# A branch after expert 0 that gives four experts two blocks instead of two, with three- and two-block experts in turn

## The chip, the cores and the metric

The kernel runs on one core of one Trainium2 chip. Its time is the device time of one execution in microseconds (us); the kernel before takes 1819.07 us, the median of 3 runs from 1818.38 to 1819.39.

## What is computed

The reference is a two-layer model over 256 latent tokens and 256 context tokens of width 1024. Layer 0 is neighbourhood attention and a dense SwiGLU; layer 1 is differential attention and a mixture of eight experts, of which each token takes two. A final RMSNorm ends it. The part that matters here is the mixture:

```python
def moe_swiglu(h, w_router, w_gate, w_up, w_down):
    logits = (h @ w_router).astype(jnp.float32)
    top_vals, top_idx = lax.top_k(logits, TOP_K)          # TOP_K = 2 of N_EXPERTS = 8
    top_w = jax.nn.softmax(top_vals, axis=-1)
    gates = jnp.sum(jax.nn.one_hot(top_idx, N_EXPERTS, dtype=jnp.float32) * top_w[..., None], axis=-2)
    y = jnp.zeros_like(h)
    for e in range(N_EXPERTS):
        y = y + gates[..., e:e + 1] * swiglu(h, w_gate[e], w_up[e], w_down[e])
    return y
```

An expert has three matrices of 1024 x 3584 in float32 (D_FF_EXPERT = 3584), 42 MB in all (an MB here is 1,048,576 bytes), and the eight of them are 336 MB of weights that are read once. 256 tokens with two experts each make 512 rows, 64 for an expert on average.

## The kernel before, in words

**Stages.** The attention of both layers and the dense SwiGLU come first; the expert stage starts at about 900 us. It computes only the rows that an expert was given. The router's choice becomes a rank of each token within its expert; `dispatch` (L1379) builds a 0/1 matrix from ranks, `gather` (L1410) multiplies the tokens by it into `xg`, and `scatter` (L1438) takes the expert's output back to the tokens' rows with the transposed matrix.

**Blocks.** An expert's rows are held in blocks of 32. `BLOCKS` (L34) gives the number of blocks for each place in the order: six experts have three blocks, 96 rows, and the last two have two blocks, 64 rows. `first_gates` (L1461) counts the tokens of each expert and sorts: expert 0 is always first, the others follow by falling count. The indices go into registers of SP (L1478), from which the loads of the later experts take their addresses. If an expert got more rows than its blocks hold, an extra pass at the end (`tc.If(over > 0)`, L1650) handles the rest.

**Matmuls.** The 32 columns of a block are the stationary side, a quarter of the array at a time, and 256 columns of weights move past them. `quarters` (L1517) writes four such matmuls, one to each quarter. A unit of weights is a tile of 128 x 2048 float32, 1 MB; each unit takes two rounds of `quarters` per block, so 8 matmuls for each block: 24 with three blocks, 16 with two. The trace records two matmuls for each of these, so a unit of a two-block expert is x32 there, and one of a three-block expert x48.

**Steps of an expert.** An expert has four steps `j` (L1564 on): three with 4 units of `egate` and 4 of `eup`, and one with 4 units of `eboth`; the down projection of a step (`edown`, 4, 4, 4 and 2 units) stands one step later, so that expert `e` does the last down projection of expert `e - 1`. That makes 42 units an expert. Between them stand the transposes of the step before (L1533), and in steps 0 to 3 the dispatch of the next expert, the two halves of the scatter of the one before, and the gather of the next. TensorE, ScalarE and VectorE follow the order in which the code is written (`tc.manual_schedule`, L1564).

**The load queue.** All weights are loaded by SP, in the order of one list of units. `raw_unit` (L250) loads as far ahead as the ring of buffers is long: 17 buffers of 1 MB in the expert stage (3 + 4 + 4 + 2 + 4, L1089, L1248, L1292). A load waits until TensorE has used the unit that lay in its buffer. Loads take eight completion semaphores in turn, and a load also waits until the one that used its semaphore before has landed, so at most eight are in flight. L206 is the load's line; a tile `w` in the rows is a unit.

**The end.** The last expert's rows go straight through `last_expert` (L1610) into `final_norm` (L1626): squares on ScalarE, products on POOL, then four output transfers, two issued by SP and two by ScalarE (L1643). Then every engine loads a register and branches over the extra pass (L1649, L1650).

Of the kernel before, what the change touches and what calls it, by code (L numbers as in the profile page):

```python
# [17 lines left out]
D = 1024  # L18
# [11 lines left out]
NE = 8  # L30
# [3 lines left out]
BLOCKS = (3, 3, 3, 3, 3, 3, 2, 2)  # L34
# [139 lines left out]
class Stream:  # L174
# [4 lines left out]
    def __init__(self, nc, units, ahead, hl_pool, n_hl):  # L179
        self.nc, self.units = nc, units  # L180
        self.index = {u[0]: i for i, u in enumerate(units)}
        self.ahead = ahead
        self.rings, self.count = {}, {}
        self.hl_pools = [(hl_pool, n_hl)] * n_hl
        self.loaded = self.split = self.offset = self.nh = 0
        self.raw, self.hl = {}, {}

    def ring(self, name, *pools):

        self.rings[name] = [p for p in pools for _ in range(p[1])]  # L190
        self.count.setdefault(name, 0)

    def load_to(self, n):
        while self.loaded < min(n, len(self.units)):
# [5 lines left out]
            ring = self.rings[name]  # L200
            pool, bufs, tag = (*ring[self.count[name] % len(ring)], "w32")[:3]
            if pool is None:
                return
            self.count[name] += 1
            t = pool.tile([128, UNIT], F32, name="w32", tag=tag, bufs=bufs)
# [4 lines left out]
    def piece(self, n):  # L210

        while self.split < min(n, len(self.units)):
# [4 lines left out]
            self.load_to(i + 1 + len(self.rings[name]))  # L217
# [51 lines left out]
def body(tc, A, out):  # L269
# [65 lines left out]
    place = []  # L335

    def at_place(n, r, u):
        if not r:
            return A[n][0, u]
        return A[n][bass.ds(place[r - 1], 1), u].rearrange("a p c -> (a p) c") if place else None  # L340

    def add_expert(n, r, u0, nu):
        for u in range(u0, u0 + nu):
            add((n, r, u), lambda u=u: at_place(n, r, u), UNIT, False)

    steps = [(e, j) for e in range(NE) for j in range(4)]
    for i in range(len(steps) + 1):
        if i < len(steps):
            e, j = steps[i]
            if j < 3:  # L350
                add_expert("egate", e, *ESTEPS[j])
                add_expert("eup", e, *ESTEPS[j])
            else:
                add_expert("eboth", e, 0, 4)
        if i:
            e, j = steps[i - 1]
            add_expert("edown", e, 4 * j, 4 if j < 3 else 2)
# [6 lines left out]
    with ExitStack() as top:  # L364
# [1012 lines left out]
        slots_of = [32 * b for b in BLOCKS]  # L1377

        def dispatch(e, r, n):  # L1379

            d = adas[:, 256 * (e % 2):256 * (e % 2) + 2 * n].rearrange("p (b s) -> p b s", b=2)
# [4 lines left out]
        def slots(e, d, n):  # L1386

            p = PT.tile(None, None, "o")
            for tb in range(2):
                PE.transpose(p[:n, 128 * tb:128 * tb + 128], d[:, tb], ident)  # L1390
            scat[e] = scats[e % 3]
            SC.copy(scat[e][:n], p[:n, :256])

        def gather_half(hf, d, u, tag, n):

            p = PT.tile(None, None, tag)
# [13 lines left out]
        def gather(e):  # L1410
            xg[e] = ep.tile([128, KC, 96], F32, name="xg", bufs=2)
            for hf in range(2):
                gather_half(hf, dis[e], xg[e], ("o", "pt")[hf], slots_of[e])
# [12 lines left out]
        def collect(e, pd):  # L1426

            n = slots_of[e]
            oe = ep.tile([128, D], F32, name="oe", bufs=1)
# [8 lines left out]
        def scatter(e, hf):  # L1438

            c = slice(512 * hf, 512 * hf + 512)  # L1440
            n = slots_of[e]
            for tb in range(2):
                p = PT.tile(None, None, ("o", "pt")[tb])
# [4 lines left out]


# [4 lines left out]
        dis[0] = dispatch(0, rks, slots_of[0])  # L1454
# [3 lines left out]
        cnti = mp.tile([128, 1], I32, name="cnti")  # L1458
        ordi = mp.tile([128, 8], I32, name="ordi")

        def first_gates():  # L1461
            slots(0, dis[0], slots_of[0])

            pk = PT.tile(None, None, "o")
# [12 lines left out]
            with nc.allow_non_contiguous_dma("registers"):  # L1477
                place.extend(nc.values_load(ordi[0:1, r:r + 1], engines=[mybir.EngineType.SP], min_val=0,  # L1478
                                            max_val=NE - 1) for r in range(1, NE))
# [31 lines left out]
            V.tensor_copy(cnti, key[:, 0, 0:1])  # L1511
# [214 lines left out]
```

## Time and profile before

| | |
|---|---|
| median of 3 runs | 1819.07 us |
| profiled execution | 1817.93 us |
| its span, first to last instruction | 1816.2 us |
| TensorE busy | 1753.1 us, 97% |
| VectorE, ScalarE, POOL busy | 812.7, 495.7, 83.6 us |
| moved by DMA | 488.77 MB, mean 269 GB/s |
| expert matmuls, gate and up (L1520) | 9856 x 379 ns |
| expert matmuls, down (L1520) | 4928 x 379 ns |
| mean granted clock of TensorE | 0.995 |

The durations of single matmuls overlap, since they are pipelined, so what a unit costs is read from the starts of the groups that follow each other, and not from the mean of 379 ns. A stage of the expert part can be limited by TensorE or by the loads, and the page's averages don't tell which; the stretches by expert and the waits do.

### The profile page before, as it was taken

What the parts mean: (1) busy time and instruction counts of PE and PEld (TensorE: products, weight loads), DVE (VectorE), ACT (ScalarE), POOL (GpSimd) and SP (SyncE); (2) the same over time, 40 slices, a digit from 0 to 9 for tenths busy, and PEclk for the clock granted to TensorE, in tenths of its full rate; (3) what the DMA queues carried; (4) which work ended last, traced back from release to release, by engine and by line L of the source; (5) the groups of instructions that cost most, each with busy time, mean ns of one, the idle gap of its engine ahead of it and who ended that gap; (6) DMA issues with size and microseconds to landing.
All of it is one profiled execution on the core that took longest, in us unless ns stands there. A gap on an engine that the chain in (4) does not pass through costs nothing. (4 is left out here: it accounts for less than half of the span.)

```text
span 1816.2 us, 46890 instructions
## 1 busy us (share of the span) xinstructions
PE 1753.1 (97%) x20841; PEld 1269.2 (70%) x20841; DVE 812.7 (45%) x1732; ACT 495.7 (27%) x971; POOL 83.6 (5%) x133
## 2 busy tenths in 40 slices
PE   6999999999999999999999999999999999999975
PEld 4888879877778899888856556556665565565632
DVE  5688778776766767899610020200211102011202
ACT  3677664422222255666300000000000000000101
POOL 0111002000000012211000000000000000000001
PEclk9999999999999999999999999999999999999998
DMA  8334344544555354222799999999999999999995
GB/s 343 120 133 140 111 151 164 185 171 172 202 185 185 135 190 169 89 72 104 294 381 394 347 394 359 372 389 350 378 362 383 378 364 373 381 375 417 418 418 217
DMA packets 70130, 488.77 MB, mean 269 GB/s; under 512 B 8128, under 2 KB 8384, under 8 KB 13856
## 3 DMA queue, kind: packets, MB, share of 16 engines
q1 hardware_dynamic: 67824, 480.06, 69.1%
q0 software_dynamic: 1808, 5.11, 0.9%
q8 instruction: 165, 2.70, 0.6%
q10 hardware_dynamic: 288, 0.52, 0.1%
q14 instruction: 45, 0.37, 0.1%
HBM read 484.62 MB, written 1.05 MB: 267 GB/s over the span
## 5 line engine op out<-in xcount | busy, mean ns | idle before, releaser
L1520 PE MATMUL ps_mm<-w,xg 128*32 128x256 f32 x9856 | 546.7, 379 | 6.5 <-DMA w<-eup 2.6
L1520 PEld LDWEIGHTS ps_mm<-w,xg 128*32 128x32 f32 x9856 | 315.9, 110 | 222.9 <-issue 5.6
L1520 PE MATMUL ps_s<-w,aT 128*32 128x256 f32 x4928 | 273.7, 379 | 6.6 <-DMA w<-edown 6.6
L1520 PEld LDWEIGHTS ps_s<-w,aT 128*32 128x32 f32 x4928 | 158.9, 110 | 116.0 <-DMA w<-edown 11.5
L360 PE MATMUL ps_mm<-hH,wHL 128*128 128x512 f32 (+1 forms) x616 | 230.7, 377 | 2.9 <-ACT hH L586 2.8
L362 PE MATMUL ps_mm<-hH,wHL 128*128 128x512 f32 (+1 forms) x616 | 228.7, 372 | 1.0 <-DVE wHL L230 1.0
L361 PE MATMUL ps_mm<-hL,wHL 128*128 128x512 f32 (+1 forms) x616 | 228.7, 373 | 0.0
L230 DVE TENSOR_TENSOR wHL<-w,wHL 128x1024 fp32r<-128x1024 f32 (+1 forms) x156 | 174.6, 1127 | 79.0 <-ACT wHL L229 78.5
L1542 DVE COPY aT<-ps_pt 128x384 f32<-128x384 f32 (+1 forms) x32 | 16.8, 524 | 431.5 <-PE ps_pt L1541 431.5
L229 ACT CAST wHL<-w 128x1024 fp32r<-128x1024 f32 (+1 forms) x156 | 149.9, 966 | 175.9 <-PE ps_mm L362 141.3
L360 PEld LDWEIGHTS ps_mm<-hH,wHL 128*128 128x128 f32 x616 | 115.3, 188 | 27.6 <-ACT hH L586 4.3
L362 PEld LDWEIGHTS ps_mm<-hH,wHL 128*128 128x128 f32 x616 | 115.6, 188 | 23.0 <-DVE wHL L230 1.5
L361 PEld LDWEIGHTS ps_mm<-hL,wHL 128*128 128x128 f32 x616 | 115.6, 188 | 20.7 <-DVE hL L587 0.9
L417 DVE SCALAR_TENSOR_TENSOR acc<-w,sil,acc 128x1024 f32<-128x1024 f32 x98 | 120.1, 1279 | 0.0
L1588 DVE TENSOR_TENSOR es<-es,ps_mm 128x512 f32<-128x512 f32 x24 | 16.5, 688 | 223.3 <-PE ps_mm L1520 223.3
L1573 ACT ACTIVATE es<-ps_mm 128x512 f32<-128x512 f32 x24 | 14.3, 598 | 336.8 <-PE ps_mm L1520 336.7
L360 PE MATMUL ps_mm<-aH,wHL 128*128 128x256 f32 (+1 forms) x264 | 85.1, 322 | 0.0
L361 PE MATMUL ps_mm<-aL,wHL 128*128 128x256 f32 (+1 forms) x264 | 85.0, 322 | 0.0
L362 PE MATMUL ps_mm<-aH,wHL 128*128 128x256 f32 (+1 forms) x264 | 84.4, 320 | 0.0
L360 PE MATMUL ps_mm<-wHL,hH 128*128 128x256 f32 x256 | 73.1, 285 | 0.9 <-DVE rt L1110 0.9
L361 PE MATMUL ps_mm<-wHL,hH 128*128 128x256 f32 x256 | 71.7, 280 | 0.1
L362 PE MATMUL ps_mm<-wHL,hL 128*128 128x256 f32 x256 | 71.6, 280 | 0.0
(301 smaller groups left out, 2170.4 us busy)
## 6 DMA issues: line engine op xcount, KB each, us to landing
w<-edown SPq DMA_DIRECT2D x112, 1024.0 KB, 7.5
w<-egate SPq DMA_DIRECT2D x96, 1024.0 KB, 7.2
w<-eup SPq DMA_DIRECT2D x96, 1024.0 KB, 7.2
w<-ada SPq DMA_DIRECT2D x48, 1024.0 KB, 4.9
w<-eboth SPq DMA_DIRECT2D x32, 1024.0 KB, 7.7
w<-qkv SPq DMA_DIRECT2D x24, 1024.0 KB, 4.9
w<-gu SPq DMA_DIRECT2D x22, 1024.0 KB, 4.9
w<-dn SPq DMA_DIRECT2D x24, 704.0 KB, 4.0
```

Source lines behind the costliest of these rows:

```text
L229: self.nc.scalar.copy(h[:, :n_], r[:, c])
L230: later(lambda: self.nc.vector.tensor_sub(l[:, :n_], r[:, c], h[:, :n_].bitcast(F32)))
L360: PE.matmul(o, sH, mH, start=start, stop=False)
L361: PE.matmul(o, sH, mL, start=False, stop=False)
L362: PE.matmul(o, sL, mH, start=False, stop=stop)
L417: V.scalar_tensor_tensor(acc[v], wk, x, acc[v], op0=OP.mult, op1=OP.add)
L1520: PE.matmul(out[32 * g:32 * g + 32, b0:b0 + 256], lhs(g), rhs[:, c0 + 256 * g:c0 + 256 * g + 256], start=start, stop=False, tile_position= ...
L1542: (SC.copy if q else V.tensor_copy)(t[:, q, :nb], p[:, :128 * nb].rearrange("p (b s) -> p b s", b=nb))
L1573: SC.activation(s[:, :512], pa, AF.Silu)
L1588: V.tensor_mul(s[:, :512], s[:, :512], pc)
```

## The change

`BLOCKS` becomes two tables, and `ORDER` says in which order the ranked experts run. Table 0 has four experts of three blocks and four of two; table 1 has six and two as before. Both orders begin with expert 0, and three- and two-block experts follow each other in turn (table 1 has fewer two-block experts to put between). Expert 0's four steps are common. Then all engines read the count of the fifth expert (`cnti[0]`) and branch: at 64 or fewer the rest of the kernel runs with table 0, else with table 1. Each side of the branch holds the code of all seven experts left, of the last one's scatter and of the final norm. So that both sides start from the same buffers, ring buffers, PSUM banks and the tiles `es`, `aT`, `xg` and `oe` are allocated once and taken by index.

```diff
-BLOCKS = (3, 3, 3, 3, 3, 3, 2, 2)
+BLOCKS = ((3, 3, 3, 3, 2, 2, 2, 2), (3, 3, 3, 3, 3, 3, 2, 2))
+ORDER = ((0, 7, 1, 6, 2, 5, 3, 4), (0, 7, 1, 2, 6, 3, 4, 5))
...
+    def buffer(self, name):
+        ring = self.rings[name]
+        i = self.count[name] % len(ring)
+        pool, bufs, tag = (*ring[i], "w32")[:3]
+        if pool is None:
+            return None
+        self.count[name] += 1
+        if (name, i) in self.fixed:
+            return self.fixed[name, i]
+        t = pool.tile([128, UNIT], F32, name="w32", tag=tag, bufs=bufs)
+        if name == "moe":
+            self.fixed[name, i] = t
+        return t
...
-            self.load_to(i + 1 + len(self.rings[name]))
+            self.load_to(i + bool(need) + len(self.rings[name]))
...
-            r0 = 0
-            while r0 < NE:
-                r1 = r0 + BLOCKS.count(BLOCKS[r0])
-                V.tensor_scalar(key[:, 4, r0:r1], key[:, 3, r0:r1], -float(slots_of[r0]), 0.0, op0=OP.add, op1=OP.max)
-                r0 = r1
+            V.tensor_copy(cnti[:, 0:1], key[:, 3, 4:5])
+            V.memset(caps[:, 0:6], 96.0)
+            V.memset(caps[:, 6:8], 64.0)
+            V.tensor_scalar(key[:, 4, 0:1], key[:, 3, 4:5], 64.0, -32.0, op0=OP.is_le, op1=OP.mult)
+            V.tensor_scalar(caps[:, 4:6], caps[:, 4:6], key[:, 4, 0:1], None, op0=OP.add)
+            V.tensor_sub(key[:, 4], key[:, 3], caps)
+            V.tensor_scalar(key[:, 4], key[:, 4], 0.0, None, op0=OP.max)
...
-        with tc.manual_schedule(engines={mybir.EngineType.PE, mybir.EngineType.Activation, mybir.EngineType.DVE}):
-            for i, (e, j) in enumerate(steps):
-                nb = BLOCKS[e]
+        def run(i0, i1):
+            for i in range(i0, i1):
+                e, j = at(i)
+                t = steps[i][0]
+                n_ = order[t + 1] if t + 1 < NE else None
+                l_ = order[t - 1] if t else None
+                nb = blocks[e]
...
-        fin = wp.tile([128, UNIT], F32, name="w32", tag="w32", bufs=2)[:, :D]
-        nc.sync.dma_start(fin, A["rows"][0:1].to_broadcast([128, D]))
-        def final_norm(y, z, halves):
+        def final_norm(y, halves):
+            fin = st.buffer("moe")[:, :D]
+            nc.sync.dma_start(fin, A["rows"][0:1].to_broadcast([128, D]))
+            z = st.buffer("moe").rearrange("p (b d) -> p b d", b=2)
...
+        first_gates()
+        with tc.manual_schedule(engines=pes):
+            run(0, 4)
+        def rest(a):
+            blocks[:], order[:] = BLOCKS[a], ORDER[a]
...
+            st.order(units[:dense_units] + expert_units(order))
+            with tc.manual_schedule(engines=pes):
+                run(4, len(steps))
+            i = len(steps) - 1
+            transposes(i)
+            down(i)
+            final_norm(y, last_expert(order[-1], pds.pop(order[-1])))
+        fourth = nc.values_load(cnti[0:1, 0:1], min_val=0, max_val=S)
+        with tc.If(fourth < 65) as few:
+            rest(0)
+        with few.Else():
+            rest(1)
-        over = nc.values_load(cnti[0:1, 0:1], min_val=0, max_val=S)
+        over = nc.values_load(cnti[0:1, 1:2], min_val=0, max_val=S)
         with tc.If(over > 0):
```

**On TensorE, the start of the second expert.** The names are the output tile, the weights (`w`, a unit) and the stationary side (`aT` or `xg`); `ps_s` is the down projection, `ps_mm` gate and up. Before:

```order
L1520 MATMUL ps_s<-w_9782,aT 32x256 x24
L1520 MATMUL ps_s<-w_9808,aT 32x256 x24
L1520 MATMUL ps_mm<-w_9846,xg 32x256 x24
L1520 MATMUL ps_mm<-w_9872,xg 32x256 x24
L1520 MATMUL ps_mm<-w_9898,xg 32x256 x24
L1520 MATMUL ps_mm<-w_9924,xg 32x256 x24
L1541 MATMUL ps_pt<-con,es 128x128 x3
```

The same place with the change, on the side of table 0:

```order
L1560 MATMUL ps_s<-w_8833,aT_9030 32x256 x24
L1560 MATMUL ps_s<-w_8835,aT_9030 32x256 x24
L1710 TENSOR_LOAD cnti
L1711 COMPARE_AND_BRANCH
L1560 MATMUL ps_mm<-w_8837,xg_9033 32x256 x16
L1560 MATMUL ps_mm<-w_8839,xg_9033 32x256 x16
L1560 MATMUL ps_mm<-w_8841,xg_9033 32x256 x16
L1560 MATMUL ps_mm<-w_8843,xg_9033 32x256 x16
L1581 MATMUL ps_pt<-con,es_9029 128x128 x3
```

The second expert now has 16 matmuls to a unit and not 24, and between it and expert 0's third down projection stand the register load and the branch. The code of table 0 follows the branch directly.

**On SP, the loads at the same place.** A row is a load into a ring buffer, an ISA row sets a register of the load's address. With the change:

```order
L224 DMA w_8831<-eup 128x2048
L224 ISA
L224 DMA w_8833<-eup 128x2048
L1710 TENSOR_LOAD cnti
L1710 ISA x2
L1717 TENSOR_LOAD cnti
L1717 ISA x2
L1711 COMPARE_AND_BRANCH
L224 ISA
L224 DMA w_8835<-eup 128x2048
L224 ISA
L224 DMA w_8837<-eup 128x2048
```

Before, nothing stands between those loads, and the register for the extra pass is loaded in expert 6. The branch is SP's place in its own list: it stands behind the load that goes into the buffer of the last unit but one which TensorE uses ahead of its own branch.

**On SP, the end.** Before, the output transfers and then one compare:

```order
L206 DMA w_17904<-edown 128x2048
L1624 DMA w_18198<-rows 128x1024
L1643 DMA out<-w_18200 128x512 x2
L1650 COMPARE_AND_BRANCH
```

With the change, the end of table 0's side, and the first rows of table 1's side, which a jump passes over before the compare at L1718 is reached:

```order
L224 DMA w_8849<-edown 128x2048
L1667 DMA w_8851<-rows 128x1024
L1684 DMA out<-w_8853 128x512 x2
L1711 UNCONDITIONAL_BRANCH
L224 ISA
L224 DMA w_8835<-eup 128x2048
```

The jump is new, and 562 rows of SP lie between it and the compare.

## Rows read from the trace of the kernel before

**Rows 1.** The page: TensorE's line, and its slices, DMA's and the rate.

```profile
PE 1753.1 (97%) x20841; PEld 1269.2 (70%) x20841; DVE 812.7 (45%) x1732; ACT 495.7 (27%) x971; POOL 83.6 (5%) x133
...
PE   6999999999999999999999999999999999999975
...
DMA  8334344544555354222799999999999999999995
GB/s 343 120 133 140 111 151 164 185 171 172 202 185 185 135 190 169 89 72 104 294 381 394 347 394 359 372 389 350 378 362 383 378 364 373 381 375 417 418 418 217
```

**Rows 2.** Stretches by expert 1, 5, 6, 7; last columns: clock, DMA share, GB/s.

```profile
1014.92:1134.13 119.21, 118.38 (x2084) 72.34 (x2080) 17.01 (x36) 8.04 (x18) 0.00 (x0) 1.00 0.96 376
...
1491.73:1610.87 119.14, 118.33 (x2083) 72.30 (x2079) 16.83 (x36) 7.93 (x18) 0.00 (x0) 1.00 0.97 372
1610.87:1695.06 84.19, 83.25 (x1437) 50.85 (x1433) 15.03 (x32) 6.14 (x14) 0.00 (x0) 1.00 1.01 412
1695.06:1781.44 86.38, 74.50 (x1243) 39.92 (x1235) 11.72 (x22) 4.49 (x9) 0.00 (x0) 1.00 1.01 418
```

**Rows 3.** TensorE in order of time: start, duration; three-block, then two-block units.

```profile
1065.48 10.54 PE L1520 MATMUL ps_s<-w,aT 128*32 128x256 f32 x192
1075.84 10.54 PE L1520 MATMUL ps_mm<-w,xg 128*32 128x256 f32 x192
...
1647.62 7.09 PE L1520 MATMUL ps_s<-w,aT 128*32 128x256 f32 x128
1654.53 7.09 PE L1520 MATMUL ps_mm<-w,xg 128*32 128x256 f32 x128
```

**Rows 4.** SP's waits, 1134 to 1253 us: total, times, longest.

```profile
SPq L206 <- PE ps_mm L1520: 58.8, 24, 6.5
```

**Rows 5.** Loads, KB and us to landing: 1134 to 1253; waits and loads after 1620.

```profile
w<-edown SPq DMA_DIRECT2D x14, 1024.0 KB, 7.1
...
SPq L206 <- DMA w<-edown: 31.4, 17, 2.0
...
w<-edown SPq DMA_DIRECT2D x10, 1024.0 KB, 19.8
```

**Rows 6.** TensorE in order of time, one unit a row; brackets: wait before it.

```profile
1728.73 1.93 PE L1520 MATMUL ps_mm<-w,xg 128*32 128x256 f32 x32 [1.78 <-DMA w<-eup]
...
1793.45 1.93 PE L1520 MATMUL ps_s<-w,aT 128*32 128x256 f32 x32 [0.46 <-DMA w<-edown]
```

**Rows 7.** Two stretches once the loads set the pace.

```profile
1620.00:1720.00 100.00, 99.87 (x1751) 60.69 (x1743) 19.97 (x41) 7.14 (x17) 0.00 (x0) 1.00 1.01 418
1720.00:1780.00 60.00, 49.08 (x784) 25.24 (x787) 5.47 (x9) 2.26 (x5) 0.00 (x0) 1.00 1.01 419
```

**Rows 8.** Lines L1478, L1649, L1650: duration ns min/median/max, first and last start.

```profile
L1478 SPq TENSOR_LOAD <-ordi x7: 263/263/472, 907.9 to 911.5; - x7
...
L1649 PEldq TENSOR_LOAD <-cnti x1: 483/483/483, 1800.1 to 1800.1; - x1
...
L1650 SPq EVENT_SEMAPHORE  x8: 17/17/17, 1814.0 to 1814.5; - x8
...
L1650 POOLq COMPARE_BRANCH  x1: 45/45/45, 1805.3 to 1805.3; - x1
L1650 POOLq EVENT_SEMAPHORE  x1: 17/17/17, 1805.8 to 1805.8; - x1
L1650 SPq COMPARE_BRANCH  x1: 53/53/53, 1809.8 to 1809.8; - x1
L1650 ACTq COMPARE_BRANCH  x1: 54/54/54, 1811.1 to 1811.1; - x1
L1650 ACTq EVENT_SEMAPHORE  x1: 17/17/17, 1814.3 to 1814.3; - x1
```

**Rows 9.** The end in order of time: a late weight load, the last outputs.

```profile
1801.63 0.33 PEld L1618 LDWEIGHTS ps_mm<-oe,oL 64*128 64x128 f32 x1 [0.52 <-issue]
...
1808.93 0.83 SPq L1643 DMA_DIRECT2D out<-w  x2
```

More of the change, by code (lines that the diff above doesn't have):

```diff
@@ L179, in __init__ @@
     def __init__(self, nc, units, ahead, hl_pool, n_hl):
-        self.nc, self.units = nc, units
-        self.index = {u[0]: i for i, u in enumerate(units)}
+        self.nc = nc
+        self.order(units)
         self.ahead = ahead
-        self.rings, self.count = {}, {}
+        self.rings, self.count, self.fixed = {}, {}, {}
         self.hl_pools = [(hl_pool, n_hl)] * n_hl
@@ L186, in __init__, with order @@
         self.raw, self.hl = {}, {}
+    def order(self, units):
+        self.units = units
+        self.index = {u[0]: i for i, u in enumerate(units)}
     def ring(self, name, *pools):
@@ L334, in body, with of_rank, expert_units, some @@
     ring = "moe"
-    place = []
-    def at_place(n, r, u):
+    expert = []
+    def of_rank(n, r, u):
         if not r:
             return A[n][0, u]
[L340 to L344, printed above, removed]
+        return A[n][bass.ds(expert[r - 1], 1), u].rearrange("a p c -> (a p) c") if expert else None
     steps = [(e, j) for e in range(NE) for j in range(4)]
[L347 to L357, printed above, removed]
+    def expert_units(order):
+        new = []
+        def some(n, r, u0, nu):
+            new.extend(((n, r, u), lambda u=u: of_rank(n, r, u), UNIT, False, "moe") for u in range(u0, u0 + nu))
+        for i in range(len(steps) + 1):
+            if i < len(steps):
+                e, j = steps[i]
+                if j < 3:
+                    some("egate", order[e], *ESTEPS[j])
+                    some("eup", order[e], *ESTEPS[j])
+                else:
+                    some("eboth", order[e], 0, 4)
+            if i:
+                e, j = steps[i - 1]
+                some("edown", order[e], 4 * j, 4 if j < 3 else 2)
+        return new
+    dense_units = len(units)
+    units += expert_units(ORDER[0])
     def mm3(o, sH, sL, mH, mL, start, stop):
@@ L1447, in scatter @@
                 add_rows(e, p, tb, c)
+        turn_of = {e: t for t, e in enumerate(order)}
         rk1 = mp.tile([128, 2, 8], F32, name="rk1")
@@ L1476, in first_gates @@
             V.tensor_copy(ordi, key[:, 2])
-            with nc.allow_non_contiguous_dma("registers"):
-                place.extend(nc.values_load(ordi[0:1, r:r + 1], engines=[mybir.EngineType.SP], min_val=0,
-                                            max_val=NE - 1) for r in range(1, NE))
+            expert.extend(nc.values_load(ordi[0:1, r:r + 1], engines=[mybir.EngineType.SP], min_val=0,
+                                         max_val=NE - 1) for r in range(1, NE))
             pm = mp.tile([128, 8, 8], F32, name="pm")
@@ L1528, in gate_up @@
                     k = 2 * (u0 + u) % KC + x
-                    for b in range(BLOCKS[e]):
+                    for b in range(blocks[e]):
                         quarters(ps[b], cols[b], lambda g: xg[e][:, k, 32 * b:32 * b + 32], r, D * x,
@@ L1578, in body @@
                     transposes(i - 1)
-                if j == 0 and e + 1 < NE:
-                    dis[e + 1] = dispatch(e + 1, rks, slots_of[e + 1])
-                    slots(e + 1, dis[e + 1], slots_of[e + 1])
-                elif j in (1, 2) and e:
-                    scatter(e - 1, j - 1)
-                elif j == 3 and e + 1 < NE:
-                    gather(e + 1)
+                if j == 0 and n_ is not None:
+                    dis[n_] = dispatch(n_, rks, slots_of(n_))
+                    slots(n_, dis[n_], slots_of(n_))
+                elif j in (1, 2) and l_ is not None:
+                    scatter(l_, j - 1)
+                elif j == 3 and n_ is not None:
+                    gather(n_)
                 if j < 3:
```

133 lines of the change are left out of this document (72 added, 61 removed).

## The prediction

> **What bounds the kernel now.** I read the page's busy times and slices first, then the stretches by expert, then TensorE's order of time, the waits of the load queue (SP), and the end. The page shows TensorE busy for 97% of the span, and from slice 21 of 40 to the last but one the DMA engines at 9 tenths as well, moving 347 to 418 GB/s [rows 1]. Two engines that are both nearly full call for a look stage by stage. In the expert stage five experts of three blocks take 119.2 us each and move about 372 GB/s. Expert 6, with two blocks, takes 84.2 us at 412 GB/s, and expert 7 takes 86.4 us at 418 GB/s with TensorE busy for only 74.5 of them [rows 2]. TensorE's clock is 1.00 throughout. TensorE's own order gives the price of one load of 1 MB ("unit", 42 to an expert): four units of a three-block expert take 10.36 us from start to start (1065.48 to 1075.84), 2.59 us a unit; four of a two-block expert 6.91 (1647.62 to 1654.53), 1.73 us a unit [rows 3]. The remaining 10 us of an expert are transposes, gather and scatter.
>
> With three blocks TensorE sets the pace: SP waits on it for a free buffer [rows 4], and a load lands 7.1 us after issue. At the end it is the other way round: SP waits on its own earlier loads, a load lands 19.8 us after issue [rows 5], and TensorE waits before unit after unit for its weights [rows 6]. Between the starts at 1728.73 and 1793.45 stand 26 units, 2.489 us each. That is the price of a unit when loads alone set the pace, and the rate says that the loads ran at it from about 1620 us on: 418 GB/s up to 1720, while TensorE still had stock, and 419 after that [rows 7]. So for long stretches I take 2.489 x 419/418 = 2.495 us.
>
> So at three blocks loads have 119.2 - 42 x 2.495 = 14.4 us to spare in each expert and lose them, because all 17 buffers of the ring are full. At two blocks TensorE is faster than the loads by 104.8 - 84.2 = 20.6 us an expert, and lives on the buffers.
>
> **What the change does to this.** The inputs are fixed by the reference. Worked out with its own router, the experts get 78, 71, 71, 61, 61, 66, 51 and 53 tokens. Expert 0 is first by rule, then 71, 71, 66, 61, 61, 53, 51: the fifth has 61, which is not over 64, so the branch with four two-block experts is taken, and no count exceeds its room (96 or 64), so the extra pass is skipped as before. Two experts lose one block of three, each 42 x (2.59 - 1.73) = 36 us of matmuls, and the experts run 3, 2, 3, 2, 3, 2, 3, 2.
>
> TensorE alone: from the start of the second expert (1014.92) to the last transposes (1781.44) it took 766.5 us. With three more three-block experts, three two-block ones and a last one at its busy time, 3 x 119.2 + 3 x 84.2 + 74.5 = 684.7, that is 81.8 less. This isn't the answer, since the loads then can't keep up.
>
> Loads alone: at 1610.87, before expert 6, TensorE had used 40 + 5 x 42 = 250 units, and the last of 336 was there at 1793.45, 182.6 us later; so some (1793.45 - 1610.87)/2.489 = 73.4 were outstanding and 12.6 lay landed and unused. Expert 7 of the change begins at 1014.92 in the same state (ring full behind a three-block expert, two blocks ahead) with 40 units used. From there loads need the same 182.6 us plus five experts' more, 210 units x 2.495 = 524.0, provided they never stop. They don't: the stock of 12.6 landed units goes to 4.4 after the first two-block expert (42 used, 84.2/2.495 = 33.8 landed), 10.2, 2.0, 7.8, 0, 5.8, then to zero in the last one. It never comes back to 12.6, where full buffers stopped loads before. With the old schedule the same five experts took 595.95 us, so the loads end 72.0 us earlier. TensorE, 81.8 earlier by itself, has some 10 us of slack, which hides the small edits inside its stages: other sizes of gather and scatter (the same matmul counts), five short VectorE instructions more while the tokens are counted (VectorE is busy 17 of 119 us in an expert [rows 2]), a load that is issued after the register loads of the order rather than ahead of them (the ring is full there, and three-block work covers it). If that cover went, each would cost no more than its own length, under 1 us.
>
> **The branch itself.** Each engine loads a register and compares after expert 0's last step; nothing waits there for another engine's present work, since the count was written some 100 us before (the order of the experts, worked out just ahead of it, is read at 907.9 us [rows 8]). The end of the old kernel has the same pair of instructions: TensorE's register load took 0.48 us, and ScalarE and SP stood 3.2 and 4.2 us from their compare to their next instruction (1811.1 to 1814.3, 1809.8 to 1814.0), while POOL, which jumps over a few instructions, went on after 0.5 [rows 8]. All those jumps were taken. The new one falls through into code that follows it, which no row shows: between nothing and 4.2 us. On TensorE the register load ran at 1800.1 while weights for matmuls issued earlier still loaded at 1801.63 [rows 8, 9], so about 1.5 us of sequencer work lies under matmuls already queued; on SP the queue holds some three loads. I take 0.5 us, next to POOL's row, and keep 0 and 4.2 for the range. Queued behind SP's compare are the next loads; behind TensorE's the matmuls of the second expert, whose late buffers would delay loads once that stock in flight is used up.
>
> In the Trainium skill, "Runtime: NRT & Kernel Launch", section "Instruction fetch mechanics", a taken branch to code outside the window being fetched stalls the sequencer, and fetching ahead is purely sequential. By it the fall-through costs nothing, and the sum is 0.5 less. The rows of taken jumps agree (0.5 us near, 3.2 to 4.2 far); no row shows a fall-through.
>
> At the end each engine now jumps over the other branch's code, and then over the extra pass as before. SP's part of that code is 562 rows long in the order of the program, so I price the jump at SP's 4.2 us, and it stands on the path: SP's last output transfer is issued at 1808.93 to 1809.76 [rows 9], its jump follows, and its last waits come behind it. Bounds: 0.5 (near) to 4.2.
>
> **Sum.** Own time of the profiled execution 1817.93 (span 1816.2 and 1.7 around it) - 72.0 + 0.5 + 4.2 = 1750.6. The median of the runs is 1.14 above that execution: 1751.8.
>
> **Rivals.** (a) The loads don't hold their pace. What decides is whether 2.495 us a unit lasts 700 us; the trace shows it for 170. The only long stretch, five experts, ran at 119.2/42 = 2.838 us a unit, 372 GB/s [rows 2]. If that were the loads' own limit over long times, 283.4 outstanding units would take 804 us, and the kernel 1014.9 + 804 + 22.8 (from the last landing to the end) + 4.7 + 2.9 = 1849, slower than before; the turning point is (1793.45 - 4.7 - 1014.92)/283.4 = 2.73 us a unit, 384 GB/s. Against it: in that stretch SP waited for buffers, not for loads [rows 4].
> The Trainium skill, "DMA: Bandwidth & Descriptors", section "Where 436 GB/s comes from", lets HBM bind loads at about 358 GB/s a core; that would be 2.93 us a unit and 1875. Rows 7 contradict it on this chip with one core at work (418 and 419 GB/s), and the page's own 425 GB/s for a 16 MB transfer does too.
> (b) The other branch is taken, if the chip's router counted otherwise or the counts came over 64: 22 blocks as before, but with the two-block experts spread so that TensorE never starves. That saves the 86.4 - 74.5 = 11.9 us of waiting, pays 4.2 for each taken jump and some 5 for a last expert of three blocks: about 1820, no change. Against it: 61 is four tokens from the limit.
> (c) The branch is dear: a fetch stall of about 4.2 us on SP and TensorE with the ring full, so the loads run dry: 1755.5.
> (d) The end's second jump is hidden or near, and loads hold 2.489: 1751.8 - 4.2 - 1.3 = 1746.
>
> **How the numbers follow.** Forecast 0.72, (c) 0.12, (d) 0.11, (a) 0.03, (b) 0.02. Own bounds of the forecast: pace 2.489 to 2.509 us (1,048,576 bytes at the 418 GB/s of [rows 7]) over 210 units, -1.3 to +2.9; the end -3.7 to 0; the branch -0.5 to +3.7: about 1746 to 1758. For pauses of the ring that I haven't seen I widen to 1744 to 1764. What can be told from no change is about 0.2%, 3.6 us. Faster 0.96, same 0.015, slower 0.025.
>
> **What would show it.** Right: the DMA row of the page at 9 in all slices from the second expert on, 412 to 420 GB/s in two- and three-block experts alike, SP waiting for loads more than for TensorE, TensorE waiting for weights near the end, and its last matmul of the last expert about 72 us earlier. SP's compare at the first branch should have its next load within 1 us, and the last instructions some 4 us later behind the outputs than before. Wrong: stretches under 400 GB/s with TensorE waiting for weights (a), five experts at 119 us (b), a gap on TensorE and in the DMA rate at about 1015 us (c), or SP waiting for buffers in three-block experts, which would mean that the ring filled and loads stopped again.

## The result, and the profile after

The changed kernel takes 1764.71 us, the median of 4 runs (1764.14 to 1766.74), against 1818.72 (1818.37 to 1819.39) for the kernel before: a ratio of 0.9705, 95% interval 0.9688 to 0.9721. The forecast was 1751.8 with a range up to 1764; the direction was right, the gain 13 us smaller than said. The profiled execution took 1764.36 us (span 1762.4), 53.6 us less than the one of before, where the sum had 67.3.

The table-0 side is taken, the experts alternate, and the page looks as forecast. TensorE's line, the slices of DMA's busy share, and its rate, to be held against [rows 1]:

```profile
PE 1684.8 (96%) x19483; PEld 1227.7 (70%) x19483; DVE 805.6 (46%) x1721; ACT 491.8 (28%) x963; POOL 83.6 (5%) x133
...
DMA  9243333644474446322569999999999999999993
GB/s 353 94 152 130 115 138 115 249 155 166 172 263 160 148 162 216 102 73 73 192 279 417 372 413 418 417 418 417 418 419 417 419 418 419 418 414 412 409 420 133
```

The stretches by expert, of the second to the fourth and of the last three (columns as in [rows 2], clock, DMA share and GB/s last):

```profile
1017.68:1102.19 84.51, 83.38 (x1438) 51.04 (x1438) 15.14 (x32) 6.25 (x14) 0.00 (x0) 1.00 1.01 416
1102.19:1221.40 119.21, 118.53 (x2086) 72.69 (x2082) 15.00 (x32) 7.93 (x18) 0.00 (x0) 1.00 1.01 418
1221.40:1305.70 84.30, 81.98 (x1401) 49.52 (x1394) 15.14 (x32) 6.21 (x14) 0.00 (x0) 1.00 1.01 418
...
1423.01:1519.70 96.69, 86.87 (x1437) 49.22 (x1430) 15.14 (x32) 6.22 (x14) 0.00 (x0) 1.00 1.01 418
1519.70:1638.90 119.20, 118.52 (x2082) 73.73 (x2086) 15.01 (x32) 7.93 (x18) 0.00 (x0) 1.00 1.01 414
1638.90:1736.16 97.26, 84.44 (x1406) 45.09 (x1398) 13.98 (x27) 4.49 (x9) 0.00 (x0) 1.00 0.94 385
```

A three-block expert still takes 119.2 us, but now at 414 to 418 GB/s and not 372 to 376. The two-block experts grow from 84.5 to 97 us, because TensorE comes to wait for weights. From 1017 to 1740 us SP waits for its own earlier loads (504 us in the first four rows) and little for TensorE (the fifth row is the largest of these), and a load lands 20.1 us after issue where it took 7.1 [rows 5]:

```profile
SPq L224 <- DMA w<-edown: 166.5, 87, 2.8
SPq L224 <- DMA w<-egate: 143.8, 72, 2.9
SPq L224 <- DMA w<-eup: 140.5, 72, 2.9
SPq L224 <- DMA w<-eboth: 52.7, 26, 2.8
SPq L224 <- PE ps_mm L1560: 31.2, 43, 3.3
```

So loads set the pace, as forecast; the pace is what came out slower. Two units for which TensorE waited, the 166th and the 336th (the last) of the expert stage:

```profile
1303.12 1.94 PE L1560 MATMUL ps_s<-w,aT 128*32 128x256 f32 x32 [0.56 <-DMA w<-edown]
...
1736.16 1.93 PE L1560 MATMUL ps_s<-w,aT 128*32 128x256 f32 x32 [0.55 <-DMA w<-edown]
```

Between these starts lie 170 units and 433.04 us, 2.547 us each, where the 26 units of [rows 6] had 2.489. Neighbouring starved units still stand 2.48 to 2.49 apart; single ones come later.

**Where the 13.7 us between sum and result lie.** The second expert starts at 1017.68 and not 1014.92 (+2.8, not in the sum). From there to the last unit's start are 718.48 us, where the sum had 1793.45 - 72.0 - 1014.92 = 706.5 (+12.0). From that start to the end of the span 26.24 us, where the sum had 22.75 + 4.2 (-0.7). The 0.5 for the branch has nothing to stand against (-0.5, below), and what lies around the span grew by 0.2.

### The profile page after: what moved, and what is told of

It is laid out like the page before. It is cut to its first block, busy times and chain, and to the rows that moved or that the text cites. A ratio compares the mean times of both kernels' runs of the same rounds, so it can differ in the third digit from the quotient of the medians.

```text
span 1762.4 us, 44182 instructions
## 1 busy us (share of the span) xinstructions
PE 1684.8 (96%) x19483; PEld 1227.7 (70%) x19483; DVE 805.6 (46%) x1721; ACT 491.8 (28%) x963; POOL 83.6 (5%) x133
## 5 line engine op out<-in xcount | busy, mean ns | idle before, releaser
L1560 PE MATMUL ps_mm<-w,xg 128*32 128x256 f32 x8960 | 500.0, 380 | 11.3 <-DMA w<-egate 6.2
L1560 PEld LDWEIGHTS ps_mm<-w,xg 128*32 128x32 f32 x8960 | 288.8, 110 | 208.8 <-DMA w<-egate 9.1
L1560 PE MATMUL ps_s<-w,aT 128*32 128x256 f32 x4480 | 251.4, 380 | 10.3 <-DMA w<-edown 10.2
L1560 PEld LDWEIGHTS ps_s<-w,aT 128*32 128x32 f32 x4480 | 143.8, 110 | 112.7 <-DMA w<-edown 19.7
## 6 DMA issues: line engine op xcount, KB each, us to landing
w<-edown SPq DMA_DIRECT2D x112, 1024.0 KB, 20.1
w<-egate SPq DMA_DIRECT2D x96, 1024.0 KB, 20.1
w<-eup SPq DMA_DIRECT2D x96, 1024.0 KB, 20.1
w<-eboth SPq DMA_DIRECT2D x32, 1024.0 KB, 20.1
```

What stands on the lines that cost most here:

```text
L1560: PE.matmul(out[32 * g:32 * g + 32, b0:b0 + 256], lhs(g), rhs[:, c0 + 256 * g:c0 + 256 * g + 256], start=start, stop=False, tile_position= ...
```

## The experiments

Each run has its time beside runs of the kernel before on its own chip, and what I read most is the time from the second expert's start to the last unit's start ("loads' time", 718.48 us in the changed kernel) and from there to the end ("tail", 26.24).

**Is it instruction fetch? Three runs on the pace.** The trace also records when each of the sixteen parts of a load has landed (its semaphore is raised sixteen times). In the changed kernel the first and the last part of a unit were 1.7 us apart at about the 60th unit and 12.3 at about the 220th; over these 160 units the first part had a pace of 2.489 us and the last of 2.554. At the latter, seven parts lie within 1.6 us, one is 4 us and eight are 10.9 to 12.3 us behind the first. So half of the DMA engines lag (the records don't name them, but the split into eight and eight stays), a unit is complete only when they are done, and the rate of the page, 418 GB/s, counts the bytes of the half that is ahead as well, and those of the fetched instructions. The packets of the instruction queues (q8 with 16 KB, q14 with 8 KB) are the only others in that time. The theory: fetching instructions, nearly all of them TensorE's, holds up half of the engines. The rivals: 2.55 is the loads' own limit over long times, or TensorE's reading of the weights gets in their way.

Fewer matmuls (`x5_fewer_matmuls`): in the seven later experts those of blocks 2 and 3 left out, but for the first round of each sum.

```diff
...
+                        if b and k and order.index(e):
+                            continue
                         quarters(ps[b], cols[b], lambda g: xg[e][:, k, 32 * b:32 * b + 32], r, D * x,
...
```

The down projection has a line of the same kind.

> In the seven later experts the matmuls of the second and third block are left out, but for the first of each sum, so part of the rows is not computed; the loads are the same. TensorE runs on average about 36 matmul instructions for a unit where it ran 80. If TensorE's instruction fetch, which goes through half of the DMA engines, slows the loads from 2.489 to 2.547 us a unit, the pace becomes about 2.489 + 0.058 x 36/80 = 2.515 and the time 1764.7 - 283 x 0.032 = about 1755. If TensorE's reading of the weights in SBUF gets in the way of the loads, the same, 1755. If 2.547 is the loads' own limit over long times: 1764.

Short matmuls (`x6_short_matmuls`): the same ones kept as instructions, with 8 columns.

```diff
-                PE.matmul(out[32 * g:32 * g + 32, b0:b0 + 256], lhs(g), rhs[:, c0 + 256 * g:c0 + 256 * g + 256],
+                PE.matmul(out[32 * g:32 * g + 32, b0:b0 + w], lhs(g), rhs[:, c0 + 256 * g:c0 + 256 * g + w],
...
+                                 256 if b == 0 or k == 0 or not order.index(e) else 8)
...
```

> As the run with fewer matmuls, but those matmuls stay as instructions and stream 8 columns instead of 256 (so part of the result is not computed): as many instructions as in the changed kernel, with less than half of the columns read. If instruction fetch slows the loads: 2.547 us a unit and 1764 as now. If the reading of weights does: 1755. If it is the loads' own limit: 1764.

Measured: fewer, 1754.60 us, ratio 0.9640 (0.9624 to 0.9656), loads' time 709.5; short, 1764.54, ratio 0.9693 (0.9677 to 0.9709), loads' time 718.8. The starts of the second expert and of the last unit, first fewer, then short:

```profile
1014.96 4.07 PE L1560 MATMUL ps_mm<-w,xg 128*32 128x256 f32 x72
...
1724.49 1.07 PE L1560 MATMUL ps_s<-w,aT 128*32 128x256 f32 x16 [1.34 <-DMA w<-edown]
```

```profile
1017.12 4.49 PE L1560 MATMUL ps_mm<-w,xg 128*32 128x256 f32 x128
...
1735.90 1.18 PE L1560 MATMUL ps_s<-w,aT 128*32 128x256 f32 x32 [1.24 <-DMA w<-edown]
```

The DMA queues from 1100 to 1700 us (packets, MB, share of 16 engines), first the changed kernel, then fewer, then short:

```profile
q1 hardware_dynamic: 34142, 248.64, 100.4%
q8 instruction: 78, 1.28, 0.9%
q14 instruction: 11, 0.09, 0.0%
```

```profile
q1 hardware_dynamic: 34486, 251.12, 100.9%
q8 instruction: 36, 0.59, 0.4%
```

```profile
q1 hardware_dynamic: 34172, 248.87, 100.4%
q8 instruction: 76, 1.25, 0.8%
```

With 46% of the q8 packets, what the pace of the last parts has above 2.489 falls from 0.063 to 0.029 us (units 60 to 330), 46% too. With as many packets and under half of the columns nothing changes. That rules out the loads' own limit (it would leave the first run at 1764) and the reading of weights (it would speed up the second). TensorE's mean granted clock fell in both (to 0.75 to 0.83 and 0.86 to 0.91 in the hundreds of us from 1100 to 1700, from 1.00); with loads setting the pace the second run shows no price of that.

The landing records show how the delay comes about. They are clearest in the run without the branch (`x1_no_branch`, below): from the 60th to the 330th unit 259 last parts come 2.49 us on average behind those of the unit before, none more than 2.65, and 11 come 3.9 to 4.1 us behind. These 11 hold 16.0 of the 17.0 us by which the 270 units exceed 2.489 us each, and 90 packets of q8 fall into that time, some eight for each late unit. That is what eight engines would give that take the packets in turn and each lose some 1.4 us by one.

Code on another engine (`x13_pool_code`), meant to tell fetch as such from other things that go with TensorE's instructions:

```diff
+                if i > 3:
+                    for _ in range(200):
+                        GP.memset(idle, 0.0)
```

> The changed kernel with 5600 tiny memsets on POOL in the expert stage (200 for each step, some 0.11 us each by POOL's small memsets at the start, 616 us in all, on a tile that nothing else uses). POOL is otherwise idle there. Their code is 358 KB, against some 1.5 MB that TensorE fetches in that time, and TensorE's instructions stay as they are. If instruction fetch as such slows the loads and POOL's goes through the same half of the DMA engines: the time from the second expert to the last unit grows by about 0.24 x 0.06 us x 283 = 4 us, 1769 us. If it goes through the other half, or if the slowing comes from TensorE's own work and not from fetches: no change, 1764.7.

```profile
q1 hardware_dynamic: 33974, 247.41, 100.1%
q8 instruction: 78, 1.28, 0.9%
q14 instruction: 41, 0.34, 0.1%
```

The whole takes 1809.31 us, ratio 0.9945 (0.9928 to 0.9961), a miss of my own making: POOL ran 638 memsets in 100 us, 157 ns each, was not done when the last expert was, and the final norm's products queued behind them. The loads' time tells what was asked: from 1018.32 to the last unit's start at 1743.36 are 725.0 us, 6.5 more than 718.5 (expected 4), with TensorE's packets unchanged and 30 more on q14. So code on another engine slows the loads too (the pace of the last parts is 2.573 against 2.552, units 60 to 330), but not through the same half, and neither of my cases had that. At about the 300th unit of this run one single part lands 15.6 us after the first, and eight others lie at 8.8 to 10.4; in the changed kernel eight lie at 12.8 to 14.5, and none behind them. By that, POOL's packets seem to have held up a ninth engine, which became the last. That 30 packets cost a third (0.021 us a unit) of what 89 cost in the changed kernel (0.063) is therefore no price per packet. The memsets' own writes come with their fetches in this run, and no run separates the two.

Short matmuls doubled (`x7_short_doubled`), meant as the other dose:

```diff
+                for _ in range(1 if w == 256 else 2):
```

> As the run with short matmuls, but each of the 8-column matmuls is issued twice (part of the result is not computed): per unit 128 instead of 80 matmul instructions on average. If instruction fetch slows the loads: 2.489 + 0.058 x 128/80 = 2.582 us a unit, 10 us more than now, 1774. If the reading of weights does, 1755; if it is the loads' own limit, 1764.

Measured 1854.69 us, ratio 1.0196 (1.0174 to 1.0217), far from every theory. In three-block experts TensorE itself stood still, between matmuls, for instructions:

```profile
1135.07 2.41 PE L1561 MATMUL ps_mm<-w,xg 128*32 128x8 f32 x128 [1.75 <-issue]
1141.29 1.50 PE L1561 MATMUL ps_mm<-w,xg 128*32 128x8 f32 x41 [3.80 <-issue]
...
1153.53 3.30 PE L1561 MATMUL ps_mm<-w,xg 128*32 128x8 f32 x128 [2.70 <-issue]
```

From the 200th to the 220th unit the loads took 3.31 us each, TensorE-bound. As a dose it says nothing. That TensorE waited for its own fetches behind the loads is likely and not shown.

**The start of the second expert.** Two runs: one line of the change put into the kernel before (`x8_loads_one_less`), and the changed kernel once more (`x14_changed_again`, no edit).

```diff
-            self.load_to(i + 1 + len(self.rings[name]))
+            self.load_to(i + bool(need) + len(self.rings[name]))
```

> The kernel before with one line of the change: a load that needs no preparation is issued after its unit's matmuls are ordered, one unit later in the program. In the changed kernel the second expert begins 2.8 us later than before (1017.68 instead of 1014.92), 1.3 us of it arising at 715 to 738 us, ahead of the experts. If this line is the cause, this kernel shows 1.3 us more at 740 us and about 1820.0; if not, 1818.7.

> The changed kernel once more. If the second expert's start at 1017.68 us (1014.92 before) belongs to the change, it shows again within some tenths of a us; if it is scatter between executions, it lies anywhere between 1014.9 and 1017.7, as it does in the other runs. From there to the last unit's start 718.5 us by either.

The old schedule with the line: 1820.18 us against 1820.30, ratio 1.0003 (0.9993 to 1.0012), though its profile has the second expert at 1017.47. The changed kernel again: 1763.36, ratio 0.9689 (0.9673 to 0.9705), the second expert at 1019.83, loads' time 718.62. Over the runs with the same code ahead of it that start lies between 1014.96 and 1019.83, and the 1014.92 of the profile of before is at the early end. So the 2.8 us lie within the scatter between executions; the line costs nothing that can be measured. The time from there to the last unit is the same within 0.2 us in the two executions of the changed kernel, and their tails are 26.24 and 25.15.

**What the branch costs.** Without it (`x1_no_branch`), and with its sides exchanged (`x2_sides_swapped`):

```diff
-        with tc.If(fourth < 65) as few:
-            rest(0)
-        with few.Else():
-            rest(1)
+        rest(0)
```

> The seven later experts follow expert 0 without a branch (table 0's code alone; the check for too many rows at the end stays). If the branch costs only its far jump at the end, this is 3.5 us faster than the changed kernel (the tail from the last unit's start to the end goes from 26.2 back to 22.8): about 1761.2 us. If the branch also delays the start of the second expert (2.8 us later than before at 1017.68), about 1758.5. If neither is on the path, 1764.7. The pace of loads stays at 2.547 us a unit by every theory.

```diff
-        with tc.If(fourth < 65) as few:
-            rest(0)
-        with few.Else():
-            rest(1)
+        with tc.If(fourth > 64) as many:
+            rest(1)
+        with many.Else():
+            rest(0)
```

> The same branch with its sides exchanged: table 1's code stands first and is jumped over at 1016 us, table 0's code stands last and runs into the end without a jump. The end gives back 3.5 us. If eight loads in flight and 12 landed units cover SP's and TensorE's jump of some 3.3 to 4.2 us, the first jump costs nothing: 1761. If each us for which SP issues nothing is lost to the loads, which set the pace for the rest of the kernel: 1764 to 1766. If TensorE's late release of buffers adds to that: up to 1769.

Without the branch: 1758.68 us, ratio 0.9673 (0.9657 to 0.9690); loads' time 718.16, tail 21.79. So the branch costs the loads 0.3 us and the end 26.24 - 21.79 = 4.45 (3.36 by the tail of 25.15); another 1.6 us of the difference is the second expert's earlier start, 1016.05, in that execution. In the changed kernel TensorE's matmuls run over the branch without a gap (start, duration; 1007.32 + 10.36 = 1017.68, the spacing of two such groups in [rows 3]), while its register load and compare pass under them:

```profile
1007.32 10.54 PE L1560 MATMUL ps_s<-w,aT 128*32 128x256 f32 x192
1017.68 7.09 PE L1560 MATMUL ps_mm<-w,xg 128*32 128x256 f32 x128
```

```profile
L1710 PEldq TENSOR_LOAD <-cnti x1: 497/497/497, 1016.8 to 1016.8; - x1
```

```profile
L1711 SPq COMPARE_BRANCH  x2: 38/45/52, 1016.9 to 1752.7; - x2
L1711 PEldq COMPARE_BRANCH  x2: 86/1689/3292, 1017.4 to 1742.5; - x2
...
L1718 PEldq COMPARE_BRANCH  x1: 4252/4252/4252, 1746.3 to 1746.3; - x1
...
L1718 SPq COMPARE_BRANCH  x1: 50/50/50, 1757.1 to 1757.1; - x1
```

(Lines L1710, L1711 and L1718, the check for too many rows: duration in ns, minimum, median and largest; first and last start.) TensorE's compare that falls through takes 86 ns, its far jump at the end 3292, and the one over the extra pass 4252. On SP the jump starts at 1752.7 and the next compare at 1757.1, 4.4 us later.

With the sides exchanged: 1765.37 us, ratio 0.9717 (0.9699 to 0.9734). The tail falls to 22.35, but at the branch TensorE stands still:

```profile
1019.71 4.90 PE L1560 MATMUL ps_mm<-w,xg 128*32 128x256 f32 x52 [4.21 <-issue]
1025.25 4.51 PE L1560 MATMUL ps_mm<-w,xg 128*32 128x256 f32 x76 [0.64 <-issue]
```

The ring is full there, the late release of buffers goes on to the loads (3.28 us a unit from the 45th to the 60th instead of 2.82, 6.9 us), and nothing won at the end is kept. By its time that is the second of my cases; but SP's own pause (its compare at 1014.6, its next load issued at 1019.3) and TensorE's late release, the third's, come together here, and the loads lost 6.9 us, more than the pause.

**What the order is worth** (`x3_order_plain`):

```diff
-ORDER = ((0, 7, 1, 6, 2, 5, 3, 4), (0, 7, 1, 2, 6, 3, 4, 5))
+ORDER = ((0, 1, 2, 3, 4, 5, 6, 7), (0, 1, 2, 3, 4, 5, 6, 7))
```

> The same blocks (four experts of three, four of two) without the alternation: 3, 3, 3, 3, 2, 2, 2, 2. With three blocks TensorE sets the pace and the ring stays full; loads set it only from the fifth expert on, at about 1017.7 + 3 x 119.2 = 1375.3 us, with 157 units outstanding. At the pace of the changed kernel, 2.547 us: 1375.3 + 401 + 26.2 + 2.0 = 1804 us. At the forecast's 2.495: 1796. If the stock or the order did not matter: 1764.7. The second figure to read is the pace over these 157 units: with two blocks alone TensorE executes 64 matmul records' worth of instructions a unit instead of a mean of 80, so if its instruction fetch is what slows the loads the pace is 2.489 + 0.058 x 0.8 = 2.535.

Measured 1798.79 us, ratio 0.9895 (0.9879 to 0.9912): 34 us more than with the alternation. Of the two edits, then, fewer blocks alone give 20 us and the order, on top of them, the other 34; the order without fewer blocks was not run. Up to the fifth expert the loads stand still for buffers, and after it they don't (columns as above, last is GB/s):

```profile
1300.00:1400.00 100.00, 99.19 (x1757) 60.93 (x1753) 13.39 (x31) 5.86 (x14) 0.00 (x0) 1.00 0.96 379
...
1500.00:1600.00 100.00, 83.19 (x1324) 44.99 (x1320) 13.01 (x28) 6.15 (x14) 0.00 (x0) 1.00 1.01 418
```

From the fifth expert's start at 1372.95 to the last unit's at 1769.81 are 396.9 us. By the landing records 180 units had landed at that start, so 156 were outstanding and took 2.544 us each. That lies between the 2.535 that I had for two-block code and the changed kernel's 2.547, and a single late unit is 1.4 us, 0.009 for each of 156; this run doesn't tell the two apart.

**Better versions.** First a two-block expert at the start, so that loads set the pace from there (`x4_two_first`), then the same with SP's register loads two steps later (`x11_two_first_late`):

```diff
-BLOCKS = ((3, 3, 3, 3, 2, 2, 2, 2), (3, 3, 3, 3, 3, 3, 2, 2))
-ORDER = ((0, 7, 1, 6, 2, 5, 3, 4), (0, 7, 1, 2, 6, 3, 4, 5))
+FIRST = 6
+BLOCKS = ((2, 3, 3, 3, 3, 2, 2, 2), (2, 3, 3, 3, 3, 3, 3, 2))
+ORDER = ((0, 1, 2, 7, 3, 6, 4, 5), (0, 1, 2, 7, 3, 6, 4, 5))
...
```

> The expert that is always first is one with 51 tokens and two blocks, not one with 78 and three; the others run 3, 3, 2, 3, 2, 3, 2. So loads set the pace from about 905 us on and do not stand still in the first expert. If they do, all 319 units outstanding then take 2.547 us each: 905.3 + 812.5 + 26.2 + 2.0 = 1746 us. If the ring fills again in the two three-block experts that follow each other, some 5 to 10 us more: 1751 to 1756. If the loads' rate falls in the first expert for another reason, no gain: 1764.

```diff
-            expert.extend(nc.values_load(ordi[0:1, r:r + 1], engines=[mybir.EngineType.SP], min_val=0,
-                                         max_val=NE - 1) for r in range(1, NE))
...
+                if i == 2:
+                    expert.extend(nc.values_load(ordi[0:1, r:r + 1], engines=[mybir.EngineType.SP], min_val=0,
+                                                 max_val=NE - 1) for r in range(1, NE))
```

> As the run with a two-block expert first, which gained 1.3 us where I expected 18; its SP waited 20.2 us for the order of the experts, which it loads into registers before any load of the expert stage, until about 917 us. Here SP loads those registers two steps later. If that wait is where the gain went, loads start about 9 us earlier and all that follows with them: 1754 us. If TensorE's own start or its release of buffers holds the loads: 1763.

The first: 1763.46 us, ratio 0.9697 (0.9681 to 0.9714), no gain. I had counted loads from 905 us on; SP issued none between 892 and 917 us, and most of that time it waited for the order of the experts (row of SP's waits, 900 to 1020 us: total, times, longest):

```profile
SPq L1519 <- DVE ordi L1518: 20.2, 1, 20.2
```

The second: 1759.10, ratio 0.9669 (0.9653 to 0.9685), 4.4 us better, half of what I expected, since SP then waits until 911.4 for TensorE to free the first buffer (the same view):

```profile
SPq L225 <- PE ps_mm L1560: 40.1, 22, 19.4
```

Then the end. The sides meet ahead of the last two steps (`x9_common_end`), and the check for too many rows moves there too (`x10_early_check`). In these two runs the second half of the last-but-one expert's output goes back to the tokens by another expert's indices, with the same instructions; `x15_one_end` is the first of them without that.

```diff
-ORDER = ((0, 7, 1, 6, 2, 5, 3, 4), (0, 7, 1, 2, 6, 3, 4, 5))
+ORDER = ((0, 6, 1, 5, 2, 4, 3, 7), (0, 6, 1, 2, 3, 4, 5, 7))
...
-                run(4, len(steps))
+                run(4, 30)
...
+            run(30, len(steps))
```

> The two sides of the branch meet before the last two steps of the last expert (the same two-block expert comes last in both tables), so the jump over the other side's code is taken 22 units before the end, where TensorE waits 0.55 us before each unit for its load and SP has eight loads in flight. If the far jump costs 4.4 us only because it stands at the very end: 1760.3 us, with the time from the last unit's start to the end back at 22. If a pause of 4 us on TensorE or SP there is passed on to the loads: 1764.

> As the common end, and the check for too many rows is moved there too: its side without an extra pass stands last in the program, so that this side's end needs no jump. Two far jumps follow each other 22 units before the end. If SP's 4.2 us from its last compare to its last waits, which the kernel before has as well, leave the path: 1756 us. If the two jumps together (8 us or more) are longer than what 0.55 us a unit can make good by the end: 1758 to 1762.

> The common end with expert 3 of the ranks last but one in both tables, so that all is computed: 1761 us, as the run with the common end.

Measured: 1761.68 us, ratio 0.9690 (0.9673 to 0.9706); 1759.21, 0.9671 (0.9655 to 0.9687); and 1762.53, 0.9692 (0.9676 to 0.9708). The tails are 23.30, 21.07 and 23.16, so 3 to 5 us leave the end, and some 1.3 to 1.9 us come back as loads' time (720.3, 719.8, 720.4). What is left for the common end alone is within the scatter: its complete version and the changed kernel, on one chip, take 1762.53 us (1761.66 to 1764.41) and 1763.36 (1760.67 to 1765.58). TensorE's compare for the far jump takes 6.5 us there and 3.3 at the end, so jumps are dearer while loads fill the DMA engines; between its matmuls one leaves 5.05 us, two 12.50 (brackets, first the common end, then the early check):

```profile
1686.07 9.01 PE L1560 MATMUL ps_mm<-w,xg 128*32 128x256 f32 x128 [5.05 <-issue]
```

```profile
1693.47 9.34 PE L1560 MATMUL ps_mm<-w,xg 128*32 128x256 f32 x128 [12.50 <-issue]
```

Last, the two-block start, late registers, common end and early check together (`x12_all_in`):

> The two-block expert first, the registers late, the common end and the early check together. If the three savings add up (9, 4.4 and 4.2 us off 1763.5): 1746 us. If only the ends count: 1755.

1753.08 us (1752.70 to 1753.50), ratio 0.9638 (0.9622 to 0.9654): the fastest, some 9 to 12 us ahead of the changed kernel by the ratios. The two savings add up as they were measured (1759.10 with the first two, and 5.5 us for the ends, would be 1753.6), not as I had expected them. The choice of the first expert is fitted to these counts; by the code, others still come out right by the extra pass, and slower; no run shows that.

## Why the prediction was right or wrong

- *What bounds the kernel, and which branch is taken.* Right. DMA at 9 tenths from the second expert on, SP waiting for loads, TensorE for weights, the table-0 side. Rival (b) fell, and (a) in the form given: no stretch of the loads-bound part up to the last expert is under 414 GB/s. With one core at work on this chip, the loads ran at 414 to 418 GB/s over 620 us. The Trainium skill's 358 GB/s for HBM's side of a core ("DMA: Bandwidth & Descriptors", section "Where 436 GB/s comes from") did not bind here.
- *Loads alone, 210 units x 2.495 us.* This step failed. The term is the right one and was mis-sized: 718.48 - 182.6 us for the 210 units make 2.552 each, 12.0 us more and nearly the whole miss. The landing records have 2.552 as well (units 60 to 330). The state from which I started was right: 54 units had landed at the second expert's start in both kernels, a stock of 14 and not of 12.6, as at 1610.87 before. I took the pace from 26 units that begin with a late one (the wait of 1.78 us in the first row of [rows 6]) and have no other behind it. In that same trace 67 units, from the landing at 1623.51 to the last at 1793.40, took 2.536 us each, with two late ones of 4.0 us among them. The rate of 418 GB/s, my check, can't show what was wrong: it counts bytes that the eight leading DMA engines moved ahead, and the instructions' own, while a unit waits for the eight that lag. Even my upper bound, 2.509 from that rate, was below what came. The queues of the kernel before, from 1100 to 1700 us, have the row that I priced at nothing, with about as many packets as in the changed kernel:

```profile
q8 instruction: 81, 1.33, 0.8%
```

- *Fetches, which the sum has at nothing.* For TensorE, which fetches, that holds: from 1017 to 1736 us no gap over 0.1 us between its matmuls is put down to issue. For loads that fill the DMA engines the runs show 0.063 us a unit, 2.5%. The Trainium skill, "Runtime: NRT & Kernel Launch", section "Instruction fetch mechanics", says that each engine fetches 16 KiB blocks through a DMA queue of its own and that the cost of crossing a block is mostly hidden. The trace agrees on the size for q8 (78 packets, 1.28 MB), while q14's packets, among them POOL's, are half that (41 packets, 0.34 MB in the run with code on POOL).
- *TensorE alone, with 10 us of slack.* Right in its use as far as it was tried: the one small edit that was run alone costs nothing (ratio 1.0003).
- *The branch, 0.5 us, bounds 0 to 4.2.* The lower bound was right: 0.3 us in the loads' time, where two executions of one kernel differ by 0.14. The exchanged sides show that the upper end was real for a taken jump (4.21 us between TensorE's matmuls); rival (c) had the stall right for the other layout and the price too low, since the loads lost 6.9 us.
- *The jump at the end, 4.2 us.* Right: 4.45 or 3.36 against the run without a branch, by two executions, and 4.4 us between SP's two compares. Rival (d), which hid it, fell.
- *The start of the second expert* was taken from one execution. It scatters by some 5 us between executions, and 2.8 us of the miss lie within that.

## What to carry to other kernels

When a forecast hangs on the pace of saturated loads, take that pace from the starts of starved units over hundreds of us, not from a clean short stretch and not from the GB/s: bytes of engines that run ahead don't help a tile that waits for all sixteen parts, and one unit in 24 that is 1.4 us late is easily missed. Count instruction fetch as traffic then: code that needs fewer instructions for the same work gives the loads time back, and POOL's code cost them time as TensorE's did. Lay the likely side of a branch so that it falls through where the pipeline is full, and try letting the sides meet ahead of the end, where a taken jump lies in part under other waits: here that gave 3 us at the end and cost the loads nearly 2; with the check moved there too, 5 and 1.3.

## What was not expected of the hardware

- Half of the sixteen parts of a load come up to 12 to 15 us behind the other half while all DMA engines are saturated, and with eight loads in flight the leaders then slow down to them: from 418 GB/s to 409 to 414 in the last slices of the page.
- A far jump held TensorE's compare for 3.3 and 4.3 us at the quiet end, for 4.6 us at 1015 us, for 6.5 us among saturated loads, and two in a row for 6.3 and 6.9 (a gap of 12.5 us between matmuls).
- Removing half of TensorE's code gave 9 us in a stage where TensorE wasn't the bound, and keeping the code while shrinking its work gave nothing.
- A late unit comes about once for every eight instruction packets (11 for 90 in the run without the branch), not spread over all units.
